# Closing part of a DeltaNet recurrence: squares of the outputs per group of four chunks, three turns per step

## Chip, cores and metric

The program runs on one core of a Trainium2 chip. The metric is device time in microseconds (us) for one execution. Five engines work side by side, each through its own queue in order: TensorE (PE, its weight loads shown as PEld), VectorE (DVE), ScalarE (ACT), GpSimd (POOL) and SyncE (SP), which here issues the transfers (DMA).

## What is computed

The reference is one layer of an encoder on an input of 2048 rows and 1024 columns in fp32. One of its two branches is a gated DeltaNet of 8 heads of 128 columns, run forward and backward over the rows and added; this is the part around the change:

```
o = chunk_gated_delta_rule(both(q, q), both(k, k), both(v, v), ...)
o = o[:b] + jnp.flip(o[b:], axis=1)
o = rmsnorm(o, dn_norm_w).reshape(b, L, DN_WIDTH) * jax.nn.silu(dn_z)
y_dn = o @ w_dn_out
```

The recurrence carries a 128x128 state `S` from chunk to chunk; its outputs for a chunk are a product with the state plus a product inside the chunk. `rmsnorm` needs the sum of squares of each row of a head's output. The other branch is a long convolution (Hyena); gates merge both, and an output projection, the residual and a last norm follow.

## The kernel before

The kernel works in stages. The stage of the change is the recurrence of the DeltaNet, `chain` (L1097 on), a generator that yields three times per step. It has 128 steps: 8 heads of 16 steps, one chunk of 128 rows per step and direction. In step `s` of a head the forward direction (0) takes chunk `s`, the backward one (1) chunk 15 - `s`. PE's main work at that time is the projection of the gates, matmuls of 128x512 at L614; `tick` advances `chain` by a turn after a fixed number of them, so that six or seven L614 matmuls stand in each step. PE's order is the order in which this code emits (`manual_schedule` for PE); the orders of ACT, DVE, POOL and SP come from a scheduler that fills them from what is emitted.

A step on PE and its partners: products of `k` with the state (`ch<-S`, L1179), from which DVE makes `R` (L1180); products of `q` with the state (`po<-S`, L1185); then `ch<-R` (L1188), from which DVE makes `Y` for the forward and ACT for the backward direction (L1193, L1191); transposes of the next `k` (`tk`, L1129), which ACT scales into `kt` (L1133); then `ch<-Y,kt` (L1200), from which DVE makes the new state `S` (L1203, a copy at L1205 in step 0), and `po<-Y` (L1208). In steps 0 to 7 ACT copies the output into `o` (L1215), in steps 8 to 15 DVE adds it (L1217); DVE adds the part of the state (L1219). Loads for two steps ahead (`kvq`, `ep`) are issued on SP, and POOL scales `k` (L1123).

From step 8 on an output chunk is whole, and ACT takes its squares with the row sums into `msq` (L1222), two chunks per step. After step 11 two groups of four chunks are whole (the middle of the head), after step 15 the other two. For such a pair `finish` runs, group A, then B:

- a load of the sums of squares of `q` into `sc` (two buffers) and two small operations on DVE (L1140, L1141), the second with `msq`; a power on POOL (L1142); a load of `z`, the gate (one buffer);
- ACT scales the four chunks in place (L1147);
- PE transposes them (`tr`, L1151, in one PSUM buffer that it shares with `tk`), DVE multiplies by `z` into `og` (L1153), SP stores it.

These are three turns per group, and one turn is taken at the end of each step; what is left at step 15 is run through there. After the last step the row blocks of `og` are loaded back (`rf`), split by ACT (L206) and others into two parts, and the out-projection (L1280) begins. "Head end" below is the stretch from step 15 of a head to step 2 of the next, "mid-head" steps 12 to 14.

Of the kernel before, what the change touches and what calls it, by code (L numbers as in the profile page):

```python
# [11 lines left out]
F32 = mybir.dt.float32  # L12
F32R = mybir.dt.float32r
AF = mybir.ActivationFunctionType
# [142 lines left out]
class Ring:  # L157
# [6 lines left out]
    def next(self):  # L164
        t = self.t[self.i % len(self.t)]
        self.i += 1
        return t


class K:  # L170
# [926 lines left out]
    def chain(self, P, pp, kvq, ep, sqd, sz_dram, og_dram):  # L1097

        nc = self.nc
        N = H * NCH  # L1100
        for n in ("eg", "gt", "es"):
            setattr(self, n, P.tile([128, NCH, 16], F32, name=n))
        self.kn = P.tile([128, H, NCH], F32, name="kn")
        nc.gpsimd.memset(self.kn, 0.5)
        nc.gpsimd.tensor_tensor(self.kn, self.ss, self.kn, op=ALU.pow)
        g = self.g
        for d in range(2):
            ds_ = slice(8 * d, 8 * d + 8)
            for m, o in ((self.mi[d], self.eg), (self.msr[:, d], self.es), (self.ones, self.gt)):
                ps = pp.tile([128, NCH, 8], F32, name="cs", tag="tr")  # L1110
                nc.tensor.matmul(ps, lhsT=m, rhs=g[:, :, ds_], start=True, stop=True)
                nc.scalar.activation(o[:, :, ds_], ps, AF.Exp)
        ops, kts = {}, {}
        at = lambda n, d: (n // NCH, n % NCH if d == 0 else NCH - 1 - n % NCH)

        def fetch(n):
            for d in range(2):
                h, c = at(n, d)
                a = P.tile([128, 3, 128], F32, name=f"kvq{d}", bufs=3)
                self.load(a, kvq[h][c])  # L1120
                b = P.tile([128, 2, 128], F32, name=f"ep{d}", bufs=3)
                self.load(b, ep[h][d, c])
                nc.gpsimd.tensor_scalar(a[:, 1], a[:, 1], self.kn[:, h, c:c + 1], None, op0=ALU.mult)  # L1123
                ops[n, d] = (a[:, 0], a[:, 1], a[:, 2], b[:, 0], b[:, 1])

        def turn(n):
            ps = pp.tile([128, 2, 128], F32, name="tk", tag="tr")
            for d in range(2):
                nc.tensor.transpose(ps[:, d], ops[n, d][0], self.ident)  # L1129
            for d in range(2):  # L1130
                h, c = at(n, d)
                kts[n, d] = P.tile([128, 128], F32, name=f"kt{d}", bufs=2)
                nc.scalar.activation(kts[n, d], ps[:, d], AF.Copy, scale=self.es[:, c, 8 * d + h:8 * d + h + 1])  # L1133

        def finish(h, g, o, msq):

            cs = slice(4 * g, 4 * g + 4)
            sc = P.tile([128, 4], F32, name="sc", bufs=2)
            self.load(sc, sqd[h, 512 * g:512 * g + 512].rearrange("(c p) -> p c", p=128))
            nc.vector.tensor_scalar(sc, sc, EPS, 128.0 * EPS, op0=ALU.add, op1=ALU.mult)  # L1140
            nc.vector.scalar_tensor_tensor(sc, msq, 1.0 / 128.0, sc, op0=ALU.mult, op1=ALU.add)  # L1141
            nc.gpsimd.tensor_tensor(sc, sc, self.mhalf[:, :4], op=ALU.pow)  # L1142
            z = P.tile([128, 512], F32, name="z")
            self.load(z, sz_dram[h, :, 512 * g:512 * g + 512])
            yield
            for j in range(4):
                nc.scalar.activation(o[:, j], o[:, j], AF.Copy, scale=sc[:, j:j + 1])  # L1147
            yield
            ps = pp.tile([128, 4, 128], F32, name="tr", tag="tr")
            for j in range(4):  # L1150
                nc.tensor.transpose(ps[:, j], o[:, j], self.ident)  # L1151
            og = P.tile([128, 512], F32, name="og")
            nc.vector.tensor_tensor(og, ps.rearrange("p a b -> p (a b)"), z, op=ALU.mult)  # L1153
            self.store(og_dram[h, :, 512 * g:512 * g + 512], og)
            yield

        fin = iter(())
        fetch(0)
        fetch(1)
        turn(0)  # L1160
        for n in range(N):
            h, s = n // NCH, n % NCH
            if s == 0:
                St, O, M = [None, None], {}, {}
            if n + 2 < N:
                fetch(n + 2)
            info = []
            for d in range(2):
                c = at(n, d)[1]
                ci = slice(8 * d + h, 8 * d + h + 1)  # L1170
                k, vr, q, e, p = ops.pop((n, d))
                ps = pp.tile([128, 3, 128], F32, name=f"ch{d}")
                po = pp.tile([128, 2, 128], F32, name="po", bufs=3)
                info.append((c, ci, k, vr, q, e, p, ps, po))
            R, Y = [None, None], [None, None]
            for d, (c, ci, k, vr, q, e, p, ps, po) in enumerate(info):
                R[d] = P.tile([128, 128], F32, name=f"R{d}")
                if s:
                    nc.tensor.matmul(ps[:, 0], lhsT=k, rhs=St[d], start=True, stop=True)  # L1179
                    nc.vector.scalar_tensor_tensor(R[d], ps[:, 0], self.eg[:, c, ci], vr, op0=ALU.mult, op1=ALU.subtract)  # L1180
                else:
                    nc.vector.tensor_scalar(R[d], vr, -1.0, None, op0=ALU.mult)
            for d, (c, ci, k, vr, q, e, p, ps, po) in enumerate(info):
                if s:
                    nc.tensor.matmul(po[:, 0], lhsT=q, rhs=St[d], start=True, stop=True)  # L1185
            yield
            for d, (c, ci, k, vr, q, e, p, ps, po) in enumerate(info):
                nc.tensor.matmul(ps[:, 1], lhsT=e, rhs=R[d], start=True, stop=True)  # L1188
                Y[d] = P.tile([128, 128], F32, name=f"Y{d}", bufs=2)
                if d:  # L1190
                    nc.scalar.activation(Y[d], ps[:, 1], AF.Copy, scale=self.an[:, c, ci])  # L1191
                else:
                    nc.vector.tensor_scalar(Y[d], ps[:, 1], self.an[:, c, ci], None, op0=ALU.mult)  # L1193
            if n + 1 < N:
                turn(n + 1)
            yield
            for d, (c, ci, k, vr, q, e, p, ps, po) in enumerate(info):
                kt = kts.pop((n, d))
                if s < NCH - 1:
                    nc.tensor.matmul(ps[:, 2], lhsT=kt, rhs=Y[d], start=True, stop=True)  # L1200
                    Sn = P.tile([128, 128], F32, name=f"S{d}", bufs=2)
                    if s:
                        nc.vector.scalar_tensor_tensor(Sn, St[d], self.gt[:, c, ci], ps[:, 2], op0=ALU.mult, op1=ALU.add)  # L1203
                    else:
                        nc.vector.tensor_copy(Sn, ps[:, 2])  # L1205
                    St[d] = Sn
            for d, (c, ci, k, vr, q, e, p, ps, po) in enumerate(info):
                nc.tensor.matmul(po[:, 1], lhsT=p, rhs=Y[d], start=True, stop=True)  # L1208
                g, j = c // 4, c % 4
                if g not in O:  # L1210
                    O[g] = P.tile([128, 4, 128], F32, name="o", bufs=6)
                    M[g] = P.tile([128, 4], F32, name="msq", bufs=6)
                o = O[g][:, j]
                if s < 8:
                    nc.scalar.activation(o, po[:, 1], AF.Copy)  # L1215
                else:
                    nc.vector.tensor_tensor(o, po[:, 1], o, op=ALU.add)  # L1217
                if s:
                    nc.vector.scalar_tensor_tensor(o, po[:, 0], self.eg[:, c, ci], o, op0=ALU.mult, op1=ALU.add)  # L1219
                if s >= 8:  # L1220
                    jk = P.tile([128, 128], F32, name="jk")
                    nc.scalar.activation(jk, o, AF.Square, accum_out=M[g][:, j:j + 1])  # L1222
            if s >= 8 and s % 4 == 3:
                for _ in fin:
                    pass

                def both(h, gs, O, M):
                    for g in gs:
                        yield from finish(h, g, O[g], M[g])

                fin = both(h, (s // 4, 3 - s // 4), dict(O), dict(M))
            next(fin, None)
            yield
        for _ in fin:
            pass
# [255 lines left out]
```

## Time and profile before

| what | us |
|---|---|
| median of 3 runs | 3565.34 (3564.03 to 3568.68) |
| profiled execution, its own time | 3556.92 |
| its span | 3555.1 |
| PE busy in the span | 3329.4 (94%) |
| DVE, ACT, POOL busy | 2082.1 (59%), 1463.8 (41%), 1392.1 (39%) |
| L614, the three costliest groups | 1042.3, 1034.8, 1034.2 |
| squares L1222: one, busy | 0.310 median, 128 of them |

The span is the profiled execution from its first to its last instruction. An engine's busy time is the sum over its instructions, and says nothing of what waits for it. The windows view gives busy time for a stretch, the waits view how long an engine stood before a line and what ended that, and the timeline gives start, length, engine, line and tiles of runs of instructions, with the idle time ahead and its releaser in brackets.

### The profile page before, as it was taken

The numbers are of one execution on the slowest core, as the hardware profiler recorded it, in microseconds if no ns is written. First come the engines' busy times: TensorE is split into PE (matmuls) and PEld (weight loads), VectorE is DVE, ScalarE is ACT, GpSimd is POOL, SyncE is SP. The second block draws the span as 40 slices with busy tenths as digits, with TensorE's granted clock in tenths as the row PEclk, the third lists the DMA queues.
The fourth block names the chain that finished last, engine by engine and source line by source line (L and its number), as shares of the span: only waits on it lengthen the run. The fifth ranks groups of instructions, "written<-read, shape, count | busy, mean of one in ns | idle before, by whom it ended". The sixth has DMA issues, their size and how long they took to land. (4 is left out here: it accounts for less than half of the span.)

```text
span 3555.1 us, 56321 instructions
## 1 busy us (share of the span) xinstructions
PE 3329.4 (94%) x18178; PEld 2778.2 (78%) x18178; DVE 2082.1 (59%) x4509; ACT 1463.8 (41%) x3587; POOL 1392.1 (39%) x1672
## 2 busy tenths in 40 slices
PE   7999999999999989889989999999998888999999
PEld 6767777788777777777777888888887766888998
DVE  7575555555324688878887341555555699535333
ACT  4334444433223445555554232444445577313221
POOL 3225555666432332233332124333335577324110
PEclk9999999999999999999999999999999999999999
DMA  4442333465312456677666554667767688895442
GB/s 128 133 111 88 103 115 95 154 196 179 95 56 65 125 143 164 162 174 170 166 162 163 128 146 132 205 204 205 205 206 225 201 274 260 288 308 183 142 144 92
DMA packets 715654, 577.31 MB, mean 162 GB/s; under 512 B 249646, under 2 KB 602818, under 8 KB 714336
## 3 DMA queue, kind: packets, MB, share of 16 engines
q1 hardware_dynamic: 715360, 573.72, 55.9%
q8 instruction: 145, 2.38, 0.3%
q14 instruction: 149, 1.22, 0.1%
HBM read 356.26 MB, written 217.25 MB: 161 GB/s over the span
## 5 line engine op out<-in xcount | busy, mean ns | idle before, releaser
L614 PE MATMUL pj<-hh,wh 128*128 128x512 f32 (+1 forms) x2592 | 1042.3, 403 | 18.9 <-DVE wh L208 9.6
L614 PE MATMUL pj<-hl,wh 128*128 128x512 f32 (+1 forms) x2592 | 1034.8, 400 | 3.5 <-POOL hl L209 2.8
L614 PE MATMUL pj<-hh,wl 128*128 128x512 f32 (+1 forms) x2592 | 1034.2, 400 | 1.1 <-POOL wl L209 1.0
L614 PEld LDWEIGHTS pj<-hh,wh 128*128 128x128 f32 x2592 | 494.9, 191 | 120.8 <-issue 13.1
L614 PEld LDWEIGHTS pj<-hh,wl 128*128 128x128 f32 x2592 | 495.2, 191 | 95.9 <-issue 7.9
L614 PEld LDWEIGHTS pj<-hl,wh 128*128 128x128 f32 x2592 | 495.5, 191 | 89.1 <-POOL hl L209 3.6
L209 POOL TENSOR_TENSOR wl<-wraw,wh 128x512 fp32r<-128x512 f32 x160 | 217.5, 1360 | 490.6 <-DVE wh L208 366.1
L1123 POOL TENSOR_SCALAR kvq<-kvq,kn 128x128 f32<-128x128 f32 x256 | 152.5, 605 | 295.4 <-DMA kvq<-kvq 60.9
L208 DVE CAST wh<-wraw 128x512 fp32r<-128x512 f32 x160 | 84.5, 528 | 162.2 <-DMA wraw<-in_wb 113.3
L635 DVE SCALAR_TENSOR_TENSOR o<-h_p,chy,o 128x512 f32<-128x512 f32 x96 | 89.4, 944 | 67.2 <-POOL h_p L627 65.6
L213 PE MATMUL pj<-rh,hh 128*128 128x256 f32 x448 | 126.8, 284 | 1.6 <-ACT rh L206 0.9
L214 PE MATMUL pj<-rl,hh 128*128 128x256 f32 x448 | 126.9, 284 | 0.5 <-POOL rl L209 0.5
L215 PE MATMUL pj<-rh,hl 128*128 128x256 f32 x448 | 126.9, 283 | 0.0
L961 POOL TENSOR_TENSOR co<-e,beta 128x512 f32<-128x512 f32 x64 | 75.6, 1182 | 126.6 <-DVE beta L957 71.4
L930 ACT ACTIVATE e<-e,cum 128x128 f32<-128x128 f32 x256 | 81.8, 390 | 104.5 <-DMA e<-cr 95.8
L1203 DVE SCALAR_TENSOR_TENSOR S<-S,gt,ch 128x128 f32<-128x128 f32 x224 | 69.0, 345 | 94.2 <-PE ch L1200 94.1
L621 ACT ACTIVATE h_p<-pj 128x512 f32<-128x512 f32 x96 | 57.3, 597 | 160.5 <-PE pj L614 149.6
L1343 POOL TENSOR_TENSOR gt<-gt,ex 128x256 f32<-128x256 f32 x64 | 47.9, 748 | 192.7 <-issue 98.7
L208 DVE CAST h<-raw 128x256 fp32r<-128x256 f32 x128 | 68.3, 547 | 89.0 <-PE pk L215 75.3
L965 ACT ACTIVATE od<-co 32x128 f32<-32x128 f32 x256 | 78.5, 307 | 94.7 <-DVE co L962 80.0
L209 POOL TENSOR_TENSOR l<-raw,h 128x256 fp32r<-128x256 f32 x128 | 99.6, 786 | 42.6 <-DVE h L208 40.9
L209 POOL TENSOR_TENSOR hl<-oraw,hh 128x512 fp32r<-128x512 f32 x48 | 62.5, 1305 | 127.2 <-ACT hh L206 126.7
(332 smaller groups left out, 7704.0 us busy)
## 6 DMA issues: line engine op xcount, KB each, us to landing
kvq<-kvq SPq DMA_DIRECT2D x256, 192.0 KB
wraw<-in_wb SPq DMA_DIRECT2D x160, 256.0 KB
ep<-ep SPq DMA_DIRECT2D x256, 128.0 KB
ru<-ev SPq DMA_DIRECT2D x64, 256.0 KB
rk<-ev SPq DMA_DIRECT2D x64, 256.0 KB
raw<-rk SPq DMA_DIRECT2D x128, 128.0 KB
kf<-ev SPq DMA_DIRECT2D x128, 128.0 KB
kvq<-th SPq DMA_DIRECT2D x64, 256.0 KB
```

Source lines behind the costliest of these rows:

```text
L208: (eng_h or nc.vector).tensor_copy(h, src)
L209: (eng_l or nc.gpsimd).tensor_tensor(l, src, h.bitcast(F32), op=ALU.subtract)
L213: nc.tensor.matmul(ps, lhsT=ah, rhs=bh, start=first, stop=False)
L214: nc.tensor.matmul(ps, lhsT=ah, rhs=bl, start=False, stop=False)
L215: nc.tensor.matmul(ps, lhsT=al, rhs=bh, start=False, stop=last)
L614: self.nc.tensor.matmul(ps, lhsT=a[:, k], rhs=b[k][:, ts_], start=k == 0 and j == 0, stop=k == 7 and j == 2)
L635: nc.vector.scalar_tensor_tensor(out, p[:, 2:514], cw[:, 2:3], out, op0=ALU.mult, op1=ALU.add)
L930: nc.scalar.activation(e[:, j], e[:, j], AF.Relu, scale=-1.0, bias=self.cum[:, d, h, 4 * g + j:4 * g + j + 1])
L961: nc.gpsimd.tensor_tensor(o, e, col(self.an, d), op=ALU.mult)
L965: nc.scalar.activation(od[blk(b)], o[blk(b), :, blk(b)], AF.Copy)
L1123: nc.gpsimd.tensor_scalar(a[:, 1], a[:, 1], self.kn[:, h, c:c + 1], None, op0=ALU.mult)
L1203: nc.vector.scalar_tensor_tensor(Sn, St[d], self.gt[:, c, ci], ps[:, 2], op0=ALU.mult, op1=ALU.add)
```

## The change

The squares leave the step and go into `finish`, at its start: four per group, with a turn after each two. `msq` is made there, with two buffers instead of six. And `chain` gives `finish` a turn at each of its own three turns in a step instead of at the last one only. A group now has five turns, so a pair is through after ten, the pair of the middle in step 14 and that of the end in step 2 of the next head.

```
@@ finish
-        def finish(h, g, o, msq):
+        def finish(h, g, o):
...
+            msq = P.tile([128, 4], F32, name="msq", bufs=2)
+            for j in range(4):
+                jk = P.tile([128, 128], F32, name="jk")
+                nc.scalar.activation(jk, o[:, j], AF.Square, accum_out=msq[:, j:j + 1])
+                if j % 2:
+                    yield
             sc = P.tile([128, 4], F32, name="sc", bufs=2)
...
@@ the loop over the steps
                 if s:
                     nc.tensor.matmul(po[:, 0], lhsT=q, rhs=St[d], start=True, stop=True)
+            next(fin, None)
             yield
...
             if n + 1 < N:
                 turn(n + 1)
+            next(fin, None)
             yield
...
-                    M[g] = P.tile([128, 4], F32, name="msq", bufs=6)
...
-                if s >= 8:
-                    jk = P.tile([128, 128], F32, name="jk")
-                    nc.scalar.activation(jk, o, AF.Square, accum_out=M[g][:, j:j + 1])
             if s >= 8 and s % 4 == 3:
                 for _ in fin:
                     pass
...
-                def both(h, gs, O, M):
+                def both(h, gs, O):
                     for g in gs:
-                        yield from finish(h, g, O[g], M[g])
-
-                fin = both(h, (s // 4, 3 - s // 4), dict(O), dict(M))
+                        yield from finish(h, g, O[g])
+
+                fin = both(h, (s // 4, 3 - s // 4), dict(O))
             next(fin, None)
             yield
```

What the engines' orders show of it, at three places. Lines move by a few: the squares are L1222 before and L1141 after, `Y` L1191/L1193 and L1198/L1200, the scalings L1147 and L1153, the two `sc` operations L1140, L1141 and L1146, L1147, the transposes L1151 and L1157, `og` L1153 and L1159. The number behind a name counts buffers.

ACT in head 4, from `Y` of step 11 to `Y` of step 13, before:

```order
L1191 ACTIVATE Y_26115<-ch_26099,beta 128x128
L1133 ACTIVATE kt_26120<-tk,es 128x128
L1133 ACTIVATE kt_26122<-tk,es 128x128
L1222 ACTIVATE jk,msq<-o 128x128 x2
L1191 ACTIVATE Y_26180<-ch_26164,beta 128x128
L1147 ACTIVATE o<-o,sc 128x128 x3
L1133 ACTIVATE kt_26185<-tk,es 128x128
L1133 ACTIVATE kt_26187<-tk,es 128x128
L1147 ACTIVATE o<-o,sc 128x128 x5
L1222 ACTIVATE jk,msq<-o 128x128 x2
L1191 ACTIVATE Y_26241<-ch_26225,beta 128x128
```

and after:

```order
L1198 ACTIVATE Y_26099<-ch_26083,beta 128x128
L1133 ACTIVATE kt_26104<-tk,es 128x128
L1133 ACTIVATE kt_26106<-tk,es 128x128
L1141 ACTIVATE jk,msq<-o 128x128 x5
L1198 ACTIVATE Y_26162<-ch_26142,beta 128x128
L1153 ACTIVATE o<-o,sc 128x128 x3
L1133 ACTIVATE kt_26167<-tk,es 128x128
L1133 ACTIVATE kt_26169<-tk,es 128x128
L1153 ACTIVATE o<-o,sc 128x128 x5
L1141 ACTIVATE jk,msq<-o 128x128
L1198 ACTIVATE Y_26234<-ch_26210,beta 128x128
```

Three squares more stand ahead of `Y` of step 12, one less ahead of that of step 13; the scalings keep their place.

DVE in head 4, from `R` of step 12 to the additions of step 13, before:

```order
L1180 SCALAR_TENSOR_TENSOR R_26227<-ch_26223,eg,kvq_26087 128x128
L1180 SCALAR_TENSOR_TENSOR R_26230<-ch_26225,eg,kvq_26092 128x128
L1193 TENSOR_SCALAR Y_26238<-ch_26223,beta 128x128
L1140 TENSOR_SCALAR sc<-sc 128x4
L1203 SCALAR_TENSOR_TENSOR S_26254<-S_26192,gt,ch_26223 128x128
L1203 SCALAR_TENSOR_TENSOR S_26257<-S_26195,gt,ch_26225 128x128
L1140 TENSOR_SCALAR sc<-sc 128x4
L1217 TENSOR_TENSOR o<-po,o 128x128 x2
```

and after:

```order
L1186 SCALAR_TENSOR_TENSOR R_26212<-ch_26208,eg,kvq_26071 128x128
L1186 SCALAR_TENSOR_TENSOR R_26215<-ch_26210,eg,kvq_26076 128x128
L1159 TENSOR_TENSOR og<-tr,z 128x512
L1146 TENSOR_SCALAR sc<-sc 128x4
L1200 TENSOR_SCALAR Y_26231<-ch_26208,beta 128x128
L1146 TENSOR_SCALAR sc<-sc 128x4
L1211 SCALAR_TENSOR_TENSOR S_26252<-S_26181,gt,ch_26208 128x128
L1211 SCALAR_TENSOR_TENSOR S_26255<-S_26184,gt,ch_26210 128x128
L1224 TENSOR_TENSOR o<-po,o 128x128 x2
```

The first `sc` operation goes from behind `Y` of step 13 to ahead of it, and `og` of group A stands ahead of both. In heads 1 and 3 the `sc` operation keeps its place behind `Y`. On PE, at the same place, the transposes of group A now stand behind the `po<-S` products of step 12. Before:

```order
L1179 MATMUL ch_26223<-S_26192,kvq_26087 128x128
L1179 MATMUL ch_26225<-S_26195,kvq_26092 128x128
L1185 MATMUL po<-S_26192,kvq_26087 128x128
L1185 MATMUL po<-S_26195,kvq_26092 128x128
L614 MATMUL pj<-hh_105,wl 128x512
L614 MATMUL pj<-hh_105,wh 128x512
L1188 MATMUL ch_26223<-R_26227,ep_26089 128x128
L1188 MATMUL ch_26225<-R_26230,ep_26094 128x128
```

and after:

```order
L1185 MATMUL ch_26208<-S_26181,kvq_26071 128x128
L1185 MATMUL ch_26210<-S_26184,kvq_26076 128x128
L1191 MATMUL po<-S_26181,kvq_26071 128x128
L1191 MATMUL po<-S_26184,kvq_26076 128x128
L1157 MATMUL tr<-masks,o 128x128 x4
L614 MATMUL pj<-hh_105,wl 128x512
L614 MATMUL pj<-hh_105,wh 128x512
L1195 MATMUL ch_26208<-R_26212,ep_26073 128x128
```

Before, they stood behind the `po<-Y` products of step 13; those of group B go from step 15 to step 14.

ACT in step 0 behind head 1, from its `Y` to that of step 1, before:

```order
L1191 ACTIVATE Y_23472<-ch_23460,beta 128x128
L1133 ACTIVATE kt_23477<-tk,es 128x128
L1133 ACTIVATE kt_23479<-tk,es 128x128
L1215 ACTIVATE o<-po 128x128 x2
L1147 ACTIVATE o<-o,sc 128x128 x8
L1191 ACTIVATE Y_23532<-ch_23516,beta 128x128
```

and after:

```order
L1198 ACTIVATE Y_23456<-ch_23440,beta 128x128
L1141 ACTIVATE jk,msq<-o 128x128
L1133 ACTIVATE kt_23461<-tk,es 128x128
L1133 ACTIVATE kt_23463<-tk,es 128x128
L1141 ACTIVATE jk,msq<-o 128x128
L1222 ACTIVATE o<-po 128x128
L1141 ACTIVATE jk,msq<-o 128x128
L1222 ACTIVATE o<-po 128x128
L1153 ACTIVATE o<-o,sc 128x128 x8
L1198 ACTIVATE Y_23529<-ch_23505,beta 128x128
```

Three squares stand among the copies and the `kt`, ahead of the eight scalings. On PE the transposes of A go from step 1 to step 0 there, those of B from step 4 to step 2; on DVE the two `sc` operations that follow stand both ahead of the `R` of step 1, the first of them ahead of both `S`; on POOL the first power goes from behind the second pair of operand scalings to behind the first of them. At the very end, behind the last step, ACT's order has one split of a row load (L206) ahead of the first scaling that stood behind the last one before.

## Rows read from the trace of the kernel before

**Rows 1.** Windows view, the recurrence: stretch, length, busy (x) by engine, clock, DMA.
```profile
2208.65:2778.40 569.75, 530.60 (x3675) 479.15 (x3674) 316.19 (x1092) 258.34 (x939) 222.85 (x316) 0.99 0.69 205
```

**Rows 2.** Windows view, sum over steps 8 to 10 of heads 0 to 5.
```profile
sum 74.27, PE 72.37 PEld 66.69 DVE 44.91 ACT 33.55 POOL 27.34; mean PE 12.06 PEld 11.11 DVE 7.49 ACT 5.59 POOL 4.56
```

**Rows 3.** Waits view, the recurrence: waiter, releaser, us in total, times, longest.
```profile
ACT jk L1222 <- DVE o L1219: 76.0, 54, 3.9
...
DVE sc L1140 <- DMA sc<-sqd: 20.0, 17, 3.2
...
PE ch L1200 <- ACT Y L1191: 12.8, 10, 2.9
```

**Rows 4.** Windows view, sum over steps 12 to 14 of all eight heads.
```profile
sum 113.49, PE 105.05 PEld 92.33 DVE 68.78 ACT 63.85 POOL 43.64; mean PE 13.13 PEld 11.54 DVE 8.60 ACT 7.98 POOL 5.45
```

**Rows 5.** Timeline, step 12 of head 0 and steps 12, 13 of head 4.
```profile
2260.76 0.38 SPq L178 DMA_DIRECT2D sc<-sqd  x1
...
2262.99 0.17 DVE L1140 TENSOR_SCALAR sc<-sc 128x4 f32<-128x4 f32 x1 [0.51 <-DMA sc<-sqd]
...
2542.91 0.61 PE L1185 MATMUL po<-S,kvq 128*128 128x128 f32 x4
...
2542.97 1.56 ACT L1147 ACTIVATE o<-o,sc 128x128 f32<-128x128 f32 x5
...
2543.42 0.37 SPq L178 DMA_DIRECT2D sc<-sqd  x1
...
2544.25 0.35 DVE L1193 TENSOR_SCALAR Y<-ch,beta 128x128 f32<-128x128 f32 x1 [0.68 <-PE ch L1188]
...
2544.43 0.30 ACT L1222 ACTIVATE jk<-o 128x128 f32<-128x128 f32 x1
...
2544.85 0.31 ACT L1222 ACTIVATE jk<-o 128x128 f32<-128x128 f32 x1
...
2545.19 0.86 PE L1200 MATMUL ch<-Y,kt 128*128 128x128 f32 x4
...
2547.78 0.17 DVE L1140 TENSOR_SCALAR sc<-sc 128x4 f32<-128x4 f32 x1 [3.18 <-DMA sc<-sqd]
```

**Rows 6.** Windows view, step 15 to step 2 behind head 1, and the sum of seven.
```profile
2341.75:2361.20 19.45, 16.26 (x111) 14.38 (x110) 9.02 (x32) 8.65 (x31) 6.71 (x10) 1.00 0.74 216
...
sum 132.60, PE 115.99 PEld 102.56 DVE 64.68 ACT 62.51 POOL 52.34; mean PE 16.57 PEld 14.65 DVE 9.24 ACT 8.93 POOL 7.48
```

**Rows 7.** Timeline, steps 0 and 1 behind head 1.
```profile
2347.91 0.61 PE L1185 MATMUL po<-S,kvq 128*128 128x128 f32 x4
...
2349.43 2.45 ACT L1147 ACTIVATE o<-o,sc 128x128 f32<-128x128 f32 x8 [2.18 <-POOL sc L1142]
...
2351.46 0.92 SPq L178 DMA_DIRECT2D sc<-sqd  x2
...
2352.18 0.49 PE L1200 MATMUL ch<-Y,kt 128*128 128x128 f32 x2 [1.84 <-ACT Y L1191]
...
2353.85 0.61 PE L1179 MATMUL ch<-S,kvq 128*128 128x128 f32 x4
...
2355.56 0.17 DVE L1140 TENSOR_SCALAR sc<-sc 128x4 f32<-128x4 f32 x1 [2.51 <-DMA sc<-sqd]
```

**Rows 8.** Timeline, step 14 of the last head and the tail behind step 15.
```profile
2776.12 0.61 PE L1208 MATMUL po<-Y,ep 128*128 128x128 f32 x4
...
2781.83 0.38 SPq L178 DMA_DIRECT2D z<-sz  x1
...
2782.68 2.44 ACT L1147 ACTIVATE o<-o,sc 128x128 f32<-128x128 f32 x8 [1.21 <-POOL sc L1142]
...
2784.81 0.32 SPq L178 DMA_DIRECT2D rf<-og  x1
...
2786.28 0.69 DVE L1153 TENSOR_TENSOR og<-tr,z 128x512 f32<-128x512 f32 x1 [4.62 <-DMA z<-sz]
...
2788.20 0.63 ACT L206 ACTIVATE hh<-rf 128x512 fp32r<-128x512 f32 x1 [3.07 <-DMA rf<-og]
```

More of the change, by code (lines that the diff above doesn't have):

```diff
@@ L1163, in chain @@
             if s == 0:
-                St, O, M = [None, None], {}, {}
+                St, O = [None, None], {}
             if n + 2 < N:
```

## Prediction

> **What bounds the kernel now.** I read the windows of the stretch that the change touches first, then its waits, then the timeline of the places where a closing part runs. The recurrence takes 569.75 us and TensorE (PE) is busy in 530.60 of them [rows 1]: 39 us of idle are all that an edit of order can win there, since no instruction is added or taken away. Where the squares stand today but no closing part runs (steps 8 to 10) PE is busy for nearly the whole length, 72.37 of 74.27 us over six heads [rows 2]. So the squares, two per step on ScalarE (ACT), cost PE nothing where they are. The waits say why: ACT stands 76.0 us in 54 stops, 1.4 us each, until a square's input is there [rows 3]; that idle is ACT's own, with PE at work. What PE does lose lies around the closing parts: 113.49 - 105.05 = 8.4 us in steps 12 to 14 of the eight heads [rows 4], and 132.60 - 115.99 = 16.6 us from step 15 of a head to step 2 of the next, seven times [rows 6]. That is 1.05 us and 2.4 us each. The change is worth what it does to these 25 us, and to the tail behind the last step, where the timeline shows ACT, PE and two loads in turn [rows 8].
>
> **The change part by part.** One square and the next start 0.42 us apart [rows 5].
>
> *Squares in steps 8 to 11.* One each in steps 8, 9 and 10 instead of two, then mostly five in a row in step 11, between the two `kt` and `Y` of step 12. Three more squares are 3 x 0.42 = 1.3 us. ACT stands 1.4 us at such a place until the newest output is there [rows 3], and the three early squares take outputs that are long done, so they fit into that stand: 0. If that cover is gone, one square's 0.42 us reaches `Y` in each of the eight heads, 3.4 us.
>
> *Transposes of group A in mid-head.* They go from behind the `po<-Y` products of step 13 to behind the `po<-S` products of step 12; PE needs the scaled outputs some 2 us earlier. In head 4 the fourth scaling ends at 2542.97 + 0.39 = 2543.36 and PE is through with the products ahead at 2542.91 + 0.61 = 2543.52 [rows 5]. They just fit: 0.
>
> *The first `sc` operation of the next group, on VectorE (DVE).* It waits for a load that is issued only when a scaling has freed the buffer. Before, it stands behind `Y` of step 13; after, in six of eight heads, ahead of it, at the end of step 12. DVE works in order, so `Y`, both `S`, the additions and `R` of step 13 queue behind it, and PE waits for `Y`. In head 4 the load was issued at 2543.42 and its user ran at 2547.78, 4.36 us later; in head 0 at 2260.76 and 2262.99, 2.23 us later [rows 5]. `Y` ran 0.83 us after the issue in head 4, its product on PE 0.59 us after `Y`'s end (2545.19 against 2544.25 + 0.35) [rows 5], and the transposes, now ahead of it, push `Y`'s input back by some 0.5. With the load at 3.3 us, the middle of the two, PE idles 3.3 - 0.83 - 0.59 - 0.5 = 1.4 us per head where it idles 1.05 now. Six heads: +2.1 us. With 2.23 the wait is 0.3 and the term 6 x (0.3 - 1.05) = -4.5; with 4.36 it is 2.4 and the term +8.1.
> The Trainium skill, page "DMA: Bandwidth & Descriptors", section "Anatomy of one DMA — SWDGE (gpsimd) path", puts the fixed part of a transfer at about 2.0 us: by that estimate the wait would be 0.1 us, this term -5.7 and the time some 3560 us. The section is on another issue path, and both loads in the rows took longer.
>
> *Head end.* The transposes of group A go from step 1 to step 0, those of B from step 4 to step 2; three squares more stand ahead of the scalings; the first power on GpSimd (POOL) comes a step earlier. In head 1 PE lost 19.45 - 16.26 = 3.2 us [rows 6]: 1.84 before the second `ch<-Y` product of step 1, because `Y` stood on ACT behind eight scalings that had waited 2.18 us for the powers, and most of the rest behind an `sc` load on DVE [rows 7]. After: ACT is free at 2349.43 - 2.18 = 2347.25, three squares make it 2348.5, four scalings (half of 2.45) 2349.8; PE is there at 2347.91 + 0.61 = 2348.5 [rows 7] and stands for 1.4 us, of which the transposes themselves fill 0.5: 0.9 lost. With PE 1.4 us later, `Y` of step 1 is not late any more. The `sc` load goes out at 2349.8 and lands 4.1 us later (2355.56 - 2351.46) at 2353.9; in the new order it stands ahead of both `S` of step 1, so the first `S` is there at 2353.9 + 0.17 + 0.35 = 2354.4. PE was free for the second `ch<-Y` product at 2352.18 - 1.84 = 2350.3, now 2351.7, and asks for `S` 2353.85 - 2352.18 = 1.7 us later at 2353.4 [rows 7]: 1.0 lost. With some 0.3 for the second `sc` operation ahead of `R`: 2.2 us, against 3.2 in this head and 2.4 in the mean. I take 7 x (2.2 - 2.4) = -1.4. Ends: 7 x (2.2 - 3.2) = -7, and +8 if half of the old wait (1.2 each) stays beside the new ones.
>
> *Queues.* The store of `og` and the load of `z` move ahead on SP with the transposes. `z` is single-buffered: the load for group B goes out behind `og` of A, and it took 2786.28 - 2781.83 = 4.45 us [rows 8]. Between the two `og` lie a step and a half, some 6 us (18 steps take 74.27 us [rows 2]), so I cost it at 0.
>
> *Tail.* The chain runs from the last mid-head `og` over two `z` loads to the first out-projection product. That `og` comes earlier: PE is through with `po<-Y` of step 14 at 2776.12 + 0.61 = 2776.7, transposes and `og` (0.6 and 0.69) make it 2778.0, and `z` goes out near 2778.4 instead of 2781.83. But ACT's order now has the split of a row load `rf` ahead of the scalings. `rf` went out 2784.81 - 2781.83 = 2.98 us after `z`, the split ran 3.39 us after that and takes 0.63 [rows 8]: 2785.4. So the scalings begin at 2785.4 instead of 2782.68; `og`, which had to wait for `z` until 2786.28, now waits for them: 2785.4 + 1.25 + 0.5 = 2787.2, with which it and all behind it are some 1.0 us later. The transposes of the mid group (0.6 us) go from PE's idle time here into a busy step. Together +1.6, ends 0 and +2.5.
>
> **Sum:** 2.1 - 1.4 + 1.6 = +2.3 us. The profiled execution took 3556.92 us, span 3555.1, so it would take 3559.2; it lies 8.4 us under the median of the runs, 3565.34. On the runs' scale: 3565.34 + 2.3 = **3567.6 us**. Ends: -4.5 - 7 + 0 = -11.5 (3553.8) and 8.1 + 8 + 2.5 = +18.6 (3583.9).
>
> **The rivals.** *Slower: the `sc` load decides.* If it lands as late as in head 4 or at head 1's end, over 4 us after its issue, `Y` of step 13 and `S` of step 1 wait for it in full: +8.1, +6 (most of the upper end at the head ends, 0.9 each) and +1.6, about +15.7: **3581**. At mid-head it decides from a landing of 0.83 + 0.59 + 0.5 + 1.05 = 3.0 us on; below that, this place is a gain. For it: DVE waits 20.0 us in 17 stops for this load already [rows 3], and its place in DVE's queue moves up while its issue does not. Against it: the 2.23 us of head 0.
> The Trainium skill speaks against this change here: the page "DMA: Bandwidth & Descriptors", section "Rules for kernel authors", says "Issue the DMA early, do compute, wait on its semaphore late", and the new order waits earlier on a transfer that is issued no earlier.
> *Faster: the old waits go and nothing follows.* PE waits 12.8 us in 10 stops for an ACT `Y` [rows 3], as behind the late scalings of head 1. If the earlier power, the extra turns and the moved transposes remove all of it and the `sc` loads stay hidden, the kernel gains 12.8 and gives the tail's 1.6 back: -11.2, **3554**. For it: the first power does come a step earlier. Against it: three squares stand ahead of the same scalings, so that a wait for `Y` is exchanged for one of PE's transposes.
> *The change does little.* ACT, DVE, POOL and SP are ordered by a scheduler that had already drawn pieces of the closing part forward; the transposes move by one or two steps, and nearly the same waits stay. Then the time is **3565**.
>
> **How the numbers follow.** A difference of 0.2%, 7.1 us, is about what a measurement of this kernel tells from no change. Chances: the forecast 0.45, of which 0.08 lies above +7.1 us by its upper ends; the slower rival 0.28; the faster 0.17, of which 0.02 falls short of 7.1; no effect 0.10. Slower is 0.28 + 0.08 = 0.36, faster 0.15, within 0.2% 0.37 + 0.10 + 0.02 = 0.49. The range goes from 3556 to 3582: down to -9, near the lower end of the sum, and up to the slower rival with 1 us of spread. It leaves out most of the faster rival and the last part of the slower one, under 2 in 10. The forecast and no effect alone hold 3559 to 3577.
>
> **What would show it.** Right: PE idle in steps 12 to 14 near 10.5 us over the eight heads, with DVE's longest wait there at the first `sc` operation ahead of `Y`; near 15 us at the head ends, with PE's transposes waiting for ACT about 0.9 us each time, and the 12.8 us for the ACT `Y` down to a few; steps 8 to 10 still without PE idle; the first out-projection product about 1 us later behind the last step. Wrong: a PE idle that shrinks at both places, an `sc` operation that finds its load landed, or squares that delay `Y` of step 12. A change of time outside the recurrence and its tail would be something that no step here holds.

## Result and profile after

The change makes the kernel slower: 3582.10 us in the median of 7 runs (3575.37 to 3592.44), against 3564.03 (3547.20 to 3568.68) for the kernel before in as many runs on the same chip. The ratio is 1.0066, with an interval of 1.005 to 1.0082. The forecast was 3567.6, the range ended at 3582.

The profiled execution took 3584.05 us, 27.1 more than the one before. Windows of the recurrence and of the tail up to the first out-projections (stretch, length, busy and count of PE, PEld, DVE, ACT, POOL; granted clock, DMA share, GB/s), after:

```profile
2215.19:2799.50 584.31, 539.36 (x3679) 486.03 (x3677) 315.05 (x1093) 254.94 (x933) 223.51 (x316) 0.98 0.67 200
2799.50:2826.00 26.50, 17.30 (x70) 12.60 (x69) 5.11 (x12) 8.63 (x26) 6.31 (x7) 0.87 0.55 158
```

The recurrence is 14.6 us longer [rows 1]. PE's idle grew by 5.8, 39.2 to 45.0, and its busy time by 8.8 for the same instructions. The other 12.6 us of the profile lie 6.5 ahead of the recurrence and the rest behind it. Kernels with identical code ahead of it reached it between 2208.7 and 2222.4 us, and what lies behind it took 773 to 792 us in kernels with identical code there, so I put no cause to those parts; the change is read from the recurrence.

A window of a step runs, here as in the rows before, from its first `ch<-R` product to that of the next step, so a step's own `ch<-S` and `po<-S` lie at the end of the window ahead. (By the code the transposes of A stand behind the `po<-S` of step 13 and of step 1, where the windows say 12 and 0.)

The parts of the recurrence, in the same windows as before: steps 8 to 10 of heads 0 to 5, steps 12 to 14 of eight heads, and step 15 to step 2 behind head 1 with the sum of seven such head ends.

```profile
sum 74.34, PE 72.32 PEld 66.66 DVE 44.91 ACT 26.29 POOL 26.31; mean PE 12.05 PEld 11.11 DVE 7.49 ACT 4.38 POOL 4.38
```
```profile
sum 120.23, PE 109.30 PEld 96.11 DVE 72.51 ACT 63.21 POOL 51.13; mean PE 13.66 PEld 12.01 DVE 9.06 ACT 7.90 POOL 6.39
```
```profile
2350.88:2371.78 20.90, 17.75 (x111) 15.86 (x110) 9.47 (x32) 9.43 (x37) 6.74 (x10) 0.92 0.74 203
...
sum 143.53, PE 122.25 PEld 106.97 DVE 65.26 ACT 67.85 POOL 51.60; mean PE 17.46 PEld 15.28 DVE 9.32 ACT 9.69 POOL 7.37
```

Steps 8 to 10 did not move, though ACT gave up 7.3 us of squares there [rows 2]. Mid-head PE idles 10.9 us instead of 8.4 [rows 4]. Head ends idle 21.3 instead of 16.6, and PE is busy 6.3 us longer in them [rows 6].

What PE and its partners wait for, from the waits view of the whole recurrence (waiter, releaser: us in total, times, longest), after:

```profile
ACT o L1153 <- POOL sc L1148: 27.1, 17, 3.7
...
DVE sc L1146 <- DMA sc<-sqd: 18.7, 18, 2.8
...
PE tr L1157 <- ACT o L1153: 14.8, 7, 3.2
...
PE ch L1208 <- ACT Y L1198: 8.5, 8, 2.2
```

The third row is new. ACT waits for POOL's power, and then PE's transposes wait 2.1 us on average for ACT, seven times, at six of the seven head ends. The wait for an ACT `Y` shrank from 12.8 to 8.5 [rows 3], at the head ends alone from 8.3 to 0.5.

The timeline behind head 1 (start, length, engine, line, operation, tiles; idle before) shows why the power is late. First SP and POOL in the kernel before, where step 15 starts at 2341.75:

```profile
2337.24 0.32 SPq L181 DMA_DIRECT2D og<-og  x1
2337.61 0.42 SPq L178 DMA_DIRECT2D z<-sz  x1
2338.14 0.86 SPq L178 DMA_DIRECT2D kvq<-kvq  x2
...
2341.07 2.59 SPq L178 DMA_DIRECT2D kvq<-kvq  x4
...
2344.88 0.60 POOL L1123 TENSOR_SCALAR kvq<-kvq,kn 128x128 f32<-128x128 f32 x1 [1.35 <-DMA kvq<-kvq]
...
2345.65 0.38 SPq L181 DMA_DIRECT2D og<-og  x1
...
2346.05 2.34 POOL L1123 TENSOR_SCALAR kvq<-kvq,kn 128x128 f32<-128x128 f32 x4 [0.57 <-PE pj L614]
...
2346.08 0.45 SPq L178 DMA_DIRECT2D z<-sz  x1
...
2348.36 2.02 POOL L1142 TENSOR_TENSOR sc<-sc,mhalf 128x4 f32<-128x4 f32 x2
```

Then SP, POOL, ACT and PE after, where step 15 starts at 2350.88:

```profile
2349.81 1.07 SPq L181 DMA_DIRECT2D og<-og  x1
2350.93 0.43 SPq L178 DMA_DIRECT2D z<-sz  x1
2351.46 1.81 SPq L178 DMA_DIRECT2D kvq<-kvq  x4
...
2357.62 1.18 POOL L1123 TENSOR_SCALAR kvq<-kvq,kn 128x128 f32<-128x128 f32 x2 [7.98 <-DMA kvq<-kvq]
2358.77 1.04 POOL L1148 TENSOR_TENSOR sc<-sc,mhalf 128x4 f32<-128x4 f32 x1
...
2359.84 1.28 ACT L1153 ACTIVATE o<-o,sc 128x128 f32<-128x128 f32 x4 [3.74 <-POOL sc L1148]
...
2360.30 1.21 PE L1157 MATMUL tr<-masks,o 128*128 128x128 f32 x4 [3.15 <-ACT o L1153]
```

The mid-head transposes of group B now come in step 14, and the store of `og` and the load of `z` that follow them stand ahead of four operand loads (`kvq`) on SP, which they followed before. These four go out 0.6 us after the start of step 15 instead of 0.7 before it, and the first is used 6.2 us after its issue (2357.62 - 2351.46) instead of 5.0 (2346.05 - 2341.07). So POOL starts on them 6.7 us into step 15 instead of 4.3. It scales operands first, then takes the power, and though two scalings instead of four stand ahead of the first power, this runs 7.9 us into step 15 (2358.77) instead of 6.6 (2348.36). Over the seven head ends the power comes 3.3 to 5.4 us after the start of step 0, where it came at 2.5 to 3.9 before.

Behind head 3, the one head end where no transpose waits, the same late power holds PE in another way. ACT's copies of the outputs stand behind the scalings, and PE's `po<-S` waits for these copies:

```profile
2503.75 1.28 ACT L1153 ACTIVATE o<-o,sc 128x128 f32<-128x128 f32 x4 [2.91 <-POOL sc L1148]
...
2505.22 0.41 ACT L1222 ACTIVATE o<-po 128x128 f32<-128x128 f32 x2
...
2505.53 0.79 PE L1191 MATMUL po<-S,kvq 128*128 128x128 f32 x2 [3.38 <-ACT o L1222]
```

One of the seven stops of the transposes, 1.74 us behind head 6, is of another kind: there a split of a weight load stands on ACT between the scalings (L206, 1.14 us of waiting for its load). The other six make 13.1 us, so 13.1 + 3.4 = 16.5 of the 21.3 us of idle at the head ends stand behind the power.

PE's clock fell behind such waits. Windows of 4 us around the wait of 3.15 us, after:

```profile
2356.50:2360.30 3.80, 0.65 (x7) 0.46 (x6) 0.61 (x2) 0.46 (x2) 2.67 (x4) 1.00 0.96 333
2360.30:2364.00 3.70, 3.70 (x16) 2.96 (x17) 1.31 (x3) 2.79 (x10) 2.88 (x5) 0.74 0.74 228
2364.00:2368.00 4.00, 4.00 (x26) 3.78 (x26) 2.19 (x8) 0.62 (x3) 0.00 (x0) 0.81 0.61 126
```

PE is busy without a gap in the last two, at a mean granted clock of 0.74 and 0.81, so partly at the lower level of 1.2 GHz. Taken step by step over the recurrence, the share of the clock not granted times the step's length adds up to 11.9 us after (six places behind a PE wait, and the first step) and to 4.7 before (two such places and the first step). These 7.2 us are most of the 8.8 by which PE's busy time grew. Not every such wait is followed by a lower clock: those of 2.29 and 2.44 us behind heads 2 and 4 were not.

### The profile page after: what moved, and what is told of

Read it like the earlier page. It is cut to its first block, busy times and chain, and to the rows that moved or that the text cites. A ratio compares the mean times of both kernels' runs of the same rounds, so it can differ in the third digit from the quotient of the medians.

```text
span 3582.3 us, 56268 instructions
## 1 busy us (share of the span) xinstructions
PE 3348.6 (93%) x18178; PEld 2796.2 (78%) x18178; DVE 2079.3 (58%) x4509; ACT 1460.8 (41%) x3587; POOL 1397.7 (39%) x1672
## 4 chain that ended last, share of the span: by engine, by line
PE 55%; DMA 16%; DVE 14%; issue 5%; ACT 4%; POOL 4%; SPq 3%; DVEq 0%; POOLq 0%; ACTq 0%
PE pj L614 31%; DMA wraw<-in_wb 2%; SPq L178 2%; DVE xi L996 2%; DVE tm L994 1%; PE pf L213 1%; PE pf L215 1%; PE pf L214 1%; DMA r<-r 1%; DMA e<-cr 1%; PE pj L215 1%; PE pj L214 1%; PE pj L213 1%; DMA kk<-kf 1%; PE pk L317 1%
```

## Experiments

Three theories stood at the start: 1, at the head end PE's transposes stand ahead of its other work and wait for scalings whose power is late; 2, the `sc` load's place in DVE's queue; 3, the squares' place on ACT. Beside each median stands the ratio to the kernel before, with its 95% interval; "recurrence" is the length of that window, "ends" and "mid" are PE's idle in the windows of [rows 6] and [rows 4].

**The two halves alone.** The three turns without moving the squares, in `chain` of the kernel before:

```
+            next(fin, None)
             yield
...
+            next(fin, None)
             yield
```

> Squares stay in the step as before; only the three turns per step are taken over. PE's transposes of group A then stand early in step 0 of the next head, those of B early in step 1. Theory 1 (the power): at a head end these transposes wait for the scalings, the scalings for the first power, and the power stands on POOL behind an operand scaling whose load is late on SP. Then PE waits even longer here than in the changed kernel, 4 to 6 us at each of seven head ends: the recurrence takes 600 us or more (570 before, 584 changed) and the kernel some 3595 us or more. Theory 2 (the sc load ahead of Y and S on DVE): the sc operations stand behind S here, so within 5 us of before, 3560 to 3570. Theory 3 (the squares that stand ahead of the scalings on ACT): no square has moved, so as before, 3560 to 3568.

It took 3629.58 us, 1.0167 [1.0143, 1.0190]; recurrence 633.57, ends 41.3, mid 27.1. Waits in it:

```profile
PE tr L1151 <- ACT o L1147: 38.9, 12, 6.9
...
PE tr L1151 <- ACT kt L1133: 19.0, 18, 2.9
```

With three turns per group the transposes are asked for a step earlier still, and wait up to 6.9 us. The squares are not needed for the loss: they are two turns of delay, and the change is better with them. In the change itself, behind head 1, ACT stands idle for the last 3.74 us ahead of the scalings, with its squares done. Theory 3 is out.

The squares in `finish`, one turn per step, which is the change without its two added calls of `next`:

> Squares per group in the closing part, but one turn per step as before. No transposes stand in step 0 or 1 of a head. Theory 1: PE waits for no scaling in its transposes at head ends; what the late power costs is a late Y on ACT where scalings stand ahead of it, 1 to 3 us per head end as before; the kernel lies at 3560 to 3575, nearer to before. Theory 2: the sc operations stand ahead of S in steps 13 and 14, so slower than before by half of the change's loss or more, 3573 or above. Theory 3: the squares are where they are in the changed kernel or in a longer burst, so all of the loss, 3580 or above.

It took 3607.56 us, 1.0101 [1.0084, 1.0119]; recurrence 600.74, ends 36.2. A miss. Five turns at one per step leave the transposes of both groups to step 15, where all that is left is run through, and a wait appears that no theory had:

```profile
PE tk L1129 <- issue: 27.4, 7, 5.3
```

The buffer that `tr` shares with `tk` is then held until `og` of B has its `z`, and the `tk` of step 0 stands behind it. Each half alone is worse than both together.

**The power, and the place of the transposes.** The change without the power on POOL:

```
-            nc.gpsimd.tensor_tensor(sc, sc, self.mhalf[:, :4], op=ALU.pow)
```

> The changed kernel with the power on POOL left out: the scaling takes the value in front of the power, so the heads' outputs are not normalised. Theory 1: the scalings at a head end start behind the squares and no longer behind POOL, the transposes wait under 0.5 us where they wait 2 to 3 us, and the recurrence goes from 584 to about 570 us or less, the kernel to 3560 to 3570. Theories 2 and 3: the loads and squares stay where they are, so the kernel stays within 4 us of the changed one, 3578 to 3586.

It took 3591.71 us, 1.0059 [1.0041, 1.0077]; recurrence 593.19, longer than with the power, while the ratio is level with the change's 1.0066. A miss. No wait of `tr` for ACT is left among the longer ones, but others stand in its place:

```profile
DVE sc L1146 <- DMA sc<-sqd: 43.6, 25, 3.9
...
PE tk L1129 <- DVE og L1158: 12.0, 5, 3.5
```

With the power gone, the scheduler put the `sc` operation further ahead on DVE, in front of `og` and `Y`. DVE in its timeline:

```profile
2365.63 0.17 DVE L1146 TENSOR_SCALAR sc<-sc 128x4 f32<-128x4 f32 x1 [3.88 <-DMA sc<-sqd]
...
2365.81 0.69 DVE L1158 TENSOR_TENSOR og<-tr,z 128x512 f32<-128x512 f32 x1
2366.42 0.34 DVE L1199 TENSOR_SCALAR Y<-ch,beta 128x128 f32<-128x128 f32 x1
```

That is theory 2's wait, at a head end. Three turns more between scalings and transposes:

```
             yield
+            for _ in range(3):
+                yield
             ps = pp.tile([128, 4, 128], F32, name="tr", tag="tr")
```

> The changed kernel with three more turns (one step) between the scalings and the transposes: transposes of A in step 1, of B in step 4 of a head, A in step 13 and B in step 15 at mid-head. Theory 1: PE has 4 us more until it needs the scaled outputs, so its waits there go (from 15.6 us over seven head ends to under 2); a late Y behind the scalings comes back as before; recurrence about 570 us, kernel 3562 to 3572. Theory 2: the sc operation stands ahead of S in step 13 still, and behind S in step 1: about half of the loss goes, 3573. Theory 3: the squares stay ahead of the scalings, 3578 or above.

It took 3571.83 us, 1.0017 [1.0002, 1.0032]; recurrence 576.56: half of the loss is back by the recurrence, three quarters by the ratio. The wait of `tr` is gone, and a wait for DVE outputs came out (`po` for `o` 11.3 us, `S` 7.0), with DVE's own wait for `sc` at 21.8. So two things delay a head end, and the second shows when the first is taken away. Here the power comes at 0.9 to 3.2 us of step 0, since with the transposes `og` and `z` of the mid-head have moved back behind the operand loads too; so this run does not tell the transposes' place from the power's time.

**The `sc` loads.** Four buffers instead of two for `sc`, in three kernels and in the one before:

> The changed kernel with four buffers for sc instead of two, so that its loads wait for no scaling and are landed when DVE comes to them; the engines' orders stay as they are. Theory 1 (transposes wait for scalings, scalings for the power, the power behind operand scalings whose loads are late): the 15 us of PE's transposes at the head ends stay, only a few us elsewhere go; recurrence 578 to 583 us (584 in the changed kernel), kernel 3574 to 3581. Theory 2 (the sc load): nearly all of the loss goes, recurrence about 570, kernel about 3565.

> The power left out, and four buffers for sc. Without the power alone, the first sc operation came to stand ahead of og and Y of step 1 on DVE, waited 3.9 us for its load there, and PE's transposes of k waited for og. If that wait alone took the place of the one for the power, it goes here: no long wait of PE is left at the head ends (idle there under 8 us instead of 21), recurrence 565 us or less, kernel 3558 or less. If something else holds PE at the head end (z, the squares, the shared PSUM buffer), the idle stays above 15 us and the kernel above 3575.

> The kernel before with four buffers for sc. PE's waits behind the sc load there are part of its 25 us of idle around the closing parts: the 6.0 us for S and the 3.4 us for the sum of o. Theory 1: these go, Y behind the late scalings (12.8 us) stays: recurrence 570 to about 563 us, kernel about 3558, 0.2% faster. Theory 2: if the sc loads were the larger part of all waits, 3550 or less. No effect: 3565, if another wait ends as late.

> The transposes a step later and four buffers for sc. The later transposes alone left 13.3 us of PE waiting for an ACT Y, 11.3 us for the sum of o and 7.0 us for S; the last two follow the sc load. They go: recurrence 576.6 to about 562 us, kernel 3556 to 3560, faster than both. If instead they move to another wait, above 3566.

The ratios are 1.0064 [1.0040, 1.0088], 1.0064 [1.0044, 1.0083], 0.9992 [0.9979, 1.0006] and 1.0003 [0.9989, 1.0017]; the first three recurrences, 585.20, 589.09 and 570.93, lie within 4.1 us of those with two buffers, the fourth is 7.2 longer (583.78). DVE's wait for `sc` stayed (18.5 us in 18 stops in the first): the scheduler issues a load further ahead as soon as a buffer is free, and then draws its user forward as well. So these runs did not test theory 2. Read as second samples of nearly the same order, they show how far the recurrences of two single profiles can lie apart: 1.2 us for the kernel before, 0.9 for the change, 4.1 without the power and 7.2 with the transposes later. A difference of a few us between two profiles shows nothing here.

One buffer per group, so that no load waits for a user. All loads then go out at the start: in the change from 2199.7 to 2226.5, where the recurrence runs from 2216.78 to 2797.72.

```
-            sc = P.tile([128, 4], F32, name="sc", bufs=2)
+            sc = P.tile([128, 4], F32, name="sc", bufs=32)
```

> The changed kernel with 32 buffers for sc: every load of it and its first operation on DVE then run before the first step, and none stands in the steps; the other orders stay. (With four buffers they stayed in the same places, only for a later group.) Theory 1 (the transposes wait for scalings that wait for the late power): PE's wait of 15 to 16 us for scalings at the head ends stays; idle in steps 12 to 14 falls from 10.9 to about 7, at the head ends from 21 to 17 or more; recurrence 575 to 581 us, kernel some 5 us under the changed one. Theory 2 (the sc loads make the loss): idle at both places falls to that of before or less (8 and 16.6), recurrence 570 or less, kernel 3567 or less.

> Power left out and all sc loads before the first step. Theory 1 with theory 2 as the wait right behind it: both gone, PE idle at the head ends under 9 us (21 in the changed kernel), no clock lost there, recurrence 560 to 566 us, kernel 3560 or less. If idle at the head ends stays above 15 us, a third thing holds PE there.

> The kernel before with all sc loads before the first step. The part of its idle that lies behind these loads goes: some 9 us of the 25 around the closing parts, and with it the clock lost there; Y behind the late scalings stays at 12 to 15 us. Recurrence 570 to 561 to 565 us, kernel 3557 to 3562. If the loads only hid another wait: 3565 as before.

> Transposes a step later than in the changed kernel and all sc loads before the first step. Of the waits of transposes_later (13.3 us for an ACT Y, 11.3 for the sum of o, 7.0 for S) the last two go, Y stays: recurrence 576 to 565 us or less, kernel 3555 to 3562, level with before_sc_at_start or ahead of it. If the squares in a burst are what costs, it stays 5 us or more behind before_sc_at_start.

| with `sc` loads at the start | median us, ratio | ends, mid |
|---|---|---|
| change | 3583.37, 1.0053 [1.0035, 1.0071] | 20.95, 5.1 |
| change without power | 3562.94, 0.9987 [0.9972, 1.0002] | 6.0, 6.4 |
| before | 3559.19, 0.9978 [0.9964, 0.9991] | 9.85, 3.5 |
| transposes later | 3554.89, 0.9975 [0.9961, 0.9989] | 12.5, 4.4 |

In the change itself the mid-head idle fell from 10.9 to 5.1, which is theory 2's share; but in the kernel before it fell from 8.4 to 3.5, so only 0.9 us of this share came with the change (with four buffers these two idles are 10.8 and 8.3, so they repeat within 0.2). The head ends stayed, and so did their wait:

```profile
PE tr L1157 <- ACT o L1153: 13.5, 6, 3.2
```

With the power left out, the same loads are worth 593.19 - 560.32 = 32.9 us of recurrence; in the change they are worth 3.4, within the spread above. The fastest kernel is the last, level with the kernel before that has the same loads: what gains there is the loads, not the change.

**What makes the power late.** With the loads at the start, first only the middle pair's transposes later, which puts `og` and `z` behind the operand loads on SP again; then POOL's scaling of operands left out:

```
+            for _ in range(3 if g in (1, 2) else 0):
+                yield
```

> sc_at_start with three more turns between scalings and transposes in the middle pair of a head only: og of its group B, its store and the next z load then stand on SP behind the operand loads of two steps ahead, as in the kernel before; the transposes at the head end stay where the change put them (A in step 0). If the power is late because og and z stand ahead of those operand loads on SP, the loads go out about 1 us earlier and land 1 to 2 us earlier, the first power runs at 2.5 to 3.9 us of step 0 instead of 3.3 to 5.4, and PE's wait for scalings at the head ends falls from 13.6 us to 5 or less; recurrence 568 to 574 us (581 without it). If the order on SP does not matter, the wait stays at 12 us or more and the recurrence at 578 or above.

```
-                nc.gpsimd.tensor_scalar(a[:, 1], a[:, 1], self.kn[:, h, c:c + 1], None, op0=ALU.mult)
```

> sc_at_start without POOL's scaling of the operands (the recurrence then works on unscaled values). The power itself stays, 1.04 us. If the power is late because it stands on POOL behind these scalings, it runs now at about 0.5 us of step 0, the scalings of group A end by 3 us, and PE's transposes wait 0.5 us or less each: wait for scalings under 3 us in all (13.6 with them), idle at the head ends near 6 to 9 us, recurrence 558 to 564, as without the power. If it is the power's own time or ACT's squares that hold the scalings, the wait stays above 8 us and the recurrence above 572.

The first took 3559.33 us, 0.9972 [0.9959, 0.9984]; recurrence 560.39 against 580.94, ends 10.8 against 20.95. The transposes at the head ends have the change's own order in it, and yet their wait is nearly gone:

```profile
PEld tr L1159 <- ACT o L1153: 7.1, 22, 1.4
...
PE tr L1159 <- ACT o L1153: 2.7, 4, 1.2
```

The operand loads go out 3.2 to 3.8 us ahead of step 0 and the power comes at 2.3 to 3.5. The second took 3558.38 us, 0.9980 [0.9966, 0.9994]; recurrence 557.43, ends 6.05, wait of `tr` 0.8 in one stop; the operand loads go out as late as in the change, and yet the power comes 0.6 us after the start of step 0. Both put the cause where the timeline of head 1 has it: loads behind `og` and `z`, then the scaling on POOL, then the power.

Last, the first edit alone, with two `sc` buffers:

> The changed kernel itself (two buffers for sc) with the transposes of the middle pair a step later, so that og and z stand behind the operand loads on SP again; everything at the head end stays as the change has it. If the change's own loss comes from that order on SP, PE's wait for scalings falls from 15.1 us to 5 or less and the recurrence from 584 to 570 us or less, as before the change; the sc loads' waits that were hidden behind the transposes come out again, so not much below 565; kernel 3562 to 3569. If the loss needs more than that, recurrence 577 or above and kernel 3575 or above.

It took 3576.06 us, 1.0027 [1.0010, 1.0045]; recurrence 585.98. A miss: the wait of `tr` fell, but the `sc` wait came out as it had without the power.

```profile
DVE sc L1146 <- DMA sc<-sqd: 27.6, 20, 3.7
...
PE po L1193 <- DVE o L1228: 8.3, 6, 2.3
...
PE ch L1187 <- DVE S L1213: 5.3, 5, 2.1
PE tr L1159 <- ACT o L1153: 4.8, 4, 1.8
```

Recurrence in us and ratio, by both edits:

| kernel | `sc` loaded in the steps | `sc` loaded at the start |
|---|---|---|
| before | 569.75, 1 | 553.54, 0.9978 |
| change | 584.31, 1.0066 | 580.94, 1.0053 |
| change without power | 593.19, 1.0059 | 560.32, 0.9987 |
| change, middle transposes later | 585.98, 1.0027 | 560.39, 0.9972 |

In the recurrence of the one profile of each, taking away the late power alone returns nothing, taking away the `sc` waits alone 3.4 us, both together 24. The ratios, from 4 to 12 runs each, are less sharp. The middle transposes alone return 0.39% of the time, the power left out alone 0.07% and the loads alone 0.13%, both inside the intervals; with the loads, the first edit returns 0.94% and the second 0.79%. Which part of the program holds the 0.39% is open, since the recurrence of that profile is no shorter.

The plainest comparison is within the right column. With the `sc` loads at the start the change is 0.75% slower than the kernel before, much the same loss as with the loads in the steps (0.66%), and the middle transposes later take all of it back. There the late power is the whole loss by the ratio. By the recurrence it is 20.6 of 27.4 us.

## Why the prediction was wrong

*Squares, steps 8 to 11: right.* In steps 8 to 10 PE's 72.32 us in 74.34 stand against 72.37 in 74.27 [rows 2]; in step 11, with the five squares in a row, PE idles 1.1 us over the eight heads, where it idled 1.3.

*First `sc` operation, mid-head: the size right, in part by luck.* The forecast was an idle of 10.5 us, it is 10.9. But the idle of step 13, where PE was to wait for `Y`, stayed: 46.40 - 39.69 = 6.7 us over the eight heads before, 43.00 - 36.16 = 6.8 after. There the waits for DVE's `Y` and `S` rose from 2.7 to 5.6 us, as forecast, and those for `o`, 2.0 us before, went. What was added lies in step 14, 0 before and 39.61 - 36.58 = 3.0 after. With the loads at the start the idle falls by 5.8 us in the change and by 4.9 in the kernel before, so about 0.9 of the 2.5 us added hang on these loads; the cause of the rest stays open.

*Head end: wrong, and this decides.* The term was -1.4; idle rose by 4.7 and busy time by 6.3. The step that failed is "the first power on GpSimd (POOL) comes a step earlier", together with the paragraph *Queues*, "so I cost it at 0". The sum let the scalings begin when ACT is through with the squares, at 2348.5, 6.8 us into step 15, and had no term for the power itself; they began 9.0 us into it (2359.84), behind 3.74 us of waiting for the power. I had found that the store of `og` and the load of `z` move ahead on SP, but asked only whether they hinder each other, not what is queued behind them. Behind them stand the operand loads, on them POOL's scaling, and behind that the power. In POOL's order the power moved forward; in time it came 1.3 us later behind head 1. The transposes were said to wait 0.9 us each; in the rows it is 2.1 on average. The part on `Y` held: its wait at the head ends fell from 8.3 to 0.5 us, though over the recurrence only from 12.8 to 8.5 and not to "a few".

*The clock: no term.* A PE wait of 2 to 3.4 us was priced at its length. In the recurrence the granted clock took 7.2 us more than before, more than the 5.8 us of new idle. This is read from rows and from kernels that differ in their waits too: 16.8 us were lost with `sc` at the start, 3.4 where the middle transposes came later as well. No run tested it by itself.

*Tail: the sign right, the size off.* From the last `ch<-R` to the first out-projection product it takes 14.35 us (2799.50 to 2813.85) instead of 13.9: +0.5, where the term was +1.6. The split of the row load does run ahead of the scalings, as forecast.

*The rivals.* The slower rival gave 3581, close to what came, but that is luck for the larger part. It had +8.1 us at mid-head, where PE's idle grew by 2.5, and neither the late power nor the 7.2 us of the clock. Its `sc` load is one of two waits at the head end, each enough to keep PE idle. Worked out on the rows, the sum is 2.5 (mid idle) + 4.7 (idle at the ends) + 7.2 (clock) + 0.5 (tail) = 14.9 us; with the recurrence's other steps the profile has 14.6 + 0.5 = 15.1, and the medians differ by 18.1 (by the ratio 23.5).

*Open:* why half of the gain of `sc` at the start (16 us of recurrence in the kernel before) does not reach the median (7.8 us by the ratio), what the loss outside the recurrence is, and why the places of the lowered clock differ from head to head. In the profile with these loads the recurrence starts 12.5 us later than in the kernel before (2221.11 against 2208.65), which lies within the spread of kernels with the same code ahead of it and so decides nothing.

## What to carry to other kernels

When work moves ahead in a queue, list what now stands behind it, and follow each such item to its last user, over engines that the change does not touch: here a store and a load that moved forward on SP delayed a power on POOL. Where two waits end at nearly the same time, taking away one can give little and can make the scheduler lengthen the other, so test them together before a theory falls, and set each kernel against a partner that differs in one of them alone. And price a PE wait of 2 us or more at more than its length where the rows show the granted clock falling behind such waits.

## What the runs showed of the hardware

An operand load that stood on SP behind a store and a load of 256 KB each had its user 6.2 us after its issue in the change. Before, the pair issued from 2338.14 on stood behind such a store and load too: its first user ran at 2342.93, at most 4.8 us after the issue, its second at 2344.88, straight behind a DMA wait, 5.9 to 6.7 us after. The four at 2341.07, without such a store and load just ahead, took at most 5.0. No run separates the bytes of the store and the load from their place in the queue.

A wait of 3.15 us on PE was followed by 7.7 us of busy time at a granted clock of 0.74 to 0.81, which is 0.26 x 3.70 + 0.19 x 4.00 = 1.7 us of full clock lost. And the loads of 2 KB into `sc` cost the recurrence 16.2 us in the kernel before as well (569.75 to 553.54 with all of them at the start), though DVE's whole wait for them was 20.0 us [rows 3] and DVE is far from busy (316.19 of 569.75 us [rows 1]).
